# Key scores of the decoded samples computed beside the prompt's dilated attention instead of beside the gate units

## The chip, the core and the metric

The kernel runs on one NeuronCore of one Trainium2 chip. Its engines are named as the profile names them: PE (TensorE, with PEld for its weight loads), DVE (VectorE), ACT (ScalarE), POOL (GpSimd) and SP (SyncE, which here issues every DMA). The metric is the device time of one execution in microseconds (us), the median of three runs; less is better. The kernel before takes 921.87 us (908.17 to 929.16).

## The reference, cut to what matters

One decoder layer takes one prompt of 1024 tokens and 8 decoded samples of 4 tokens each (32 sample tokens, 1056 columns in all). One input projection feeds three groups of heads: retention, dilated sliding-window attention (8 heads of 64) and attention into 256 memory tokens. Each group has a gate, and one output projection with a layer norm closes the layer. For the samples, the sliding-window attention reads a cache of keys and values:

```python
def _dilated_sample(q, keys, vals, wb, dil, steps):
    idx = wb + jnp.arange(T)[:, None] - dil * jnp.arange(steps + 1)[None, :]
    kg = keys[:, idx_c]
    vg = vals[:, idx_c]
    s = jnp.einsum('bthd,btnhd->bthn', q, kg).astype(F32) * (D ** -0.5)
    ...
    p = jnp.exp(s - m[..., None])
    l = p.sum(-1)
    o = jnp.einsum('bthn,btnhd->bthd', p, vg.astype(F32)) / l[..., None]
```

The change is about `s`, the scores of these cached keys. The kernel gets them in two ways: the last 128 positions of a sample on PE, and six classes of older positions, which only one of the four tokens reads, as a product of a cached key row with the query (on POOL) and a sum over 64 elements (on DVE).

## The kernel before, in words

The engines' programs are written in source order; nothing reorders them. The main loop goes through `UNITS`, each a projection of 256 columns: `mq`, `mk`, `mv` (memory), `qk` and `vr` (sliding-window queries and keys; values of both groups), `rq`, `rk` (retention), and the gates `rg`, `mg`, `sg`. `accumulate` (L213) issues a unit's matmuls, three per block of 128 rows since each factor is split into a high and a low part, and yields after every two blocks (six matmuls). At each yield `pump` gives credit to two streams of generators, `fa` and `fb`, by `RATE` (a pair for each unit, halved); a whole credit runs one step. So PE sees six or more matmuls of a unit, then a few of a stream's step, and so on.

- `fa` carries the memory attention, then `swa_prompt` (the prompt's dilated attention), then at unit `("mg", 0)` `ret_prompt` (retention in 8 chunks), `ret_sample` and `mem_sample`.
- `fb` carries what the samples need in the sliding-window group: `keys`, `softmax` and, during the output projection, `values` (all in `swa_sample`). Before the change, `keys` is added at `("mg", 0)`, so it runs beside retention; `softmax` follows in `("sg", 0)` and `("sg", 1)`.

A step of `swa_prompt` issues scores on PE (L521), mask and row maximum on DVE (L523), exp on ACT (L529). Later `factor` (L546 to L554, small DVE operations on tiles `sf`) merges the denominators of two patterns, which travel through DRAM (`st_d`, `so`), then `weigh` (L561, POOL) scales the scores, `trans` (L571, L576, PE) transposes them, and `av` (L600, PE) multiplies by the values. Query tiles `q` come back from DRAM (`hl_d`) by SP just ahead of use.

In retention, for each chunk of 128 tokens, `inner` issues PE L703 and L706, then DVE L709 (the masked scores `sm`) and an ACT copy. `outer` issues PE L723, L725, L728, an ACT copy, then DVE L735 (the state `R`) and `norm_sums`: DVE L794, L796, `rsqrt` (DVE L782, then POOL L783, a power), DVE L798. `apply` (ACT L803) of a chunk stands behind the next chunk's `outer`, and `finish` (PE transposes L747) three chunks later. `inner` of a chunk takes both buffers of pool `ps_s`, so it waits for DVE L709 of the chunk before it. DVE runs in order: whatever stands behind L798 waits for POOL's L783.

In `keys`, each of the 16 steps before the change has a POOL product L1059 on a tile of 128 x 1536 and, one step later, a DVE sum L1038:

```python
load_cl(d["swa_kc"], n + CL_LEAD)
pr = cl.pop((b, x))
product(n, K_POOL)(out=pr, in0=pr, in1=qb_t[b][:, None, :].to_broadcast([128, 3, 512]), op=ALU.mult)
```

Dense scores are PE L1046 and L1052. `softmax` calls `nc.gpsimd.partition_all_reduce` twice (L1101 maximum, L1116 sum). In the built program, POOL gets an instruction that loads another library of POOL code (MODIFY_POOL_CONFIG in the trace, a bare `ISA` row in the order of instructions) wherever the next operation isn't in the one at hand: the all-reduce is in one, the ordinary elementwise operations are in another.

Of the kernel before, what the change touches and what calls it, by code (L numbers as in the profile page):

```python
# [18 lines left out]
NS = 32  # L19
# [19 lines left out]
P_BUFS = 8  # L39
# [12 lines left out]
CL_LEAD = 1  # L52
# [43 lines left out]
def trunk_kernel(ctx: ExitStack, tc: tile.TileContext, d):  # L96
# [68 lines left out]
    def close(es):  # L165
        flush_stores()
        es.close()
# [798 lines left out]
    def swa_sample():  # L966
# [5 lines left out]
        qf, kf = one([128, 4, NS], "qf"), one([128, 4, NS], "kf")  # L972
# [4 lines left out]
        cm, mp, mx, sel = one([128, 4, 8, 2], "cm"), one([128, 64, 4], "mp"), one([128, 64, 4], "mx"), one([128, 64, 4], "sel")  # L977
# [3 lines left out]
        cl, qb_t, dn = {}, {}, {}  # L981
        HB = [(b, x) for b in range(8) for x in range(2)]

# [6 lines left out]
        def load_dense(src, b):  # L990
            if b < 8:
                dn[b] = clp.tile([128, 512], F32, tag="dn", name="dn")
# [8 lines left out]
        def product(n, pattern):  # L1001
            return (nc.gpsimd if pattern[n % len(pattern)] else nc.vector).tensor_tensor

        def keys():
            load(qf, qs_d[:, 0:64].rearrange("u p t c -> (p t) u c"))
            load(kf, qs_d[:, 64:128].rearrange("u p t c -> (p t) u c"))
            for n in range(CL_LEAD):
                load_cl(d["swa_kc"], n)
            load_dense(d["swa_kd"], 0)
            load_dense(d["swa_kd"], 1)  # L1010
# [6 lines left out]
            load_qb(0)  # L1017
            load_qb(1)
# [10 lines left out]
            for u in range(4):  # L1029
                nc.vector.tensor_tensor(out=En[:, u].rearrange("p b (g i) -> p b g i", g=2), in0=sn[0:NS, u * 64:(u + 1) * 64].rearrange("p (b g i) -> p b g i", b=8, g=2),  # L1030
                                        in1=mask_n[:, :, None, :].to_broadcast([NS, 8, 2, 4]), op=ALU.add)
            yield
            last = None

            def reduce():
                if last is not None:
                    b, x, pr = last
                    nc.vector.tensor_reduce(out=Ec[:, b, 3 * x:3 * x + 3].rearrange("p c h -> p (c h)"),  # L1038
                                            in_=pr.rearrange("p c (h e) -> p (c h) e", e=64), axis=AX.X, op=ALU.add)

            for n, (b, x) in enumerate(HB):
                reduce()
                if x == 0:
# [5 lines left out]
                elif b % 4 == 3:  # L1049
# [11 lines left out]
                if x == 1:  # L1061
                    load_dense(d["swa_kd"], b + 2)
                    load_qb(b + 2)
# [31 lines left out]
        def softmax():  # L1095
            nc.vector.tensor_tensor(out=Ec, in0=Ec, in1=mask_c[:, None, :, None].to_broadcast([128, 8, 6, 8]), op=ALU.add)
# [38 lines left out]
        def values():  # L1135
            for n in range(V_LEAD):
                load_cl(d["swa_vc"], n)
            load_dense(d["swa_vd"], 0)
            load_dense(d["swa_vd"], 1)
# [12 lines left out]
            for n, (b, x) in enumerate(HB):  # L1152
                if x == 0:
                    for u in range(4):
                        nc.tensor.matmul(out_of(b, u), lhsT=quarter(EdU, b, u), rhs=dn[b][:, u * 128:(u + 1) * 128], start=False, stop=False)
                    load_dense(d["swa_vd"], b + 2)
# [7 lines left out]
            ut = one([128, 4, NS], "ssu")  # L1164
# [181 lines left out]

    avail = set()
    v_used = {}
    for u, (kind, j) in enumerate(UNITS):
# [4 lines left out]
        if (kind, j) == ("vr", 0):  # L1354
# [3 lines left out]
            swa_es = ExitStack()  # L1358
# [24 lines left out]
        if (kind, j) == ("mg", 0):  # L1383
            fa.drain()
            close(swa_es)
            ret_es, cl_es, ms_es = ExitStack(), ExitStack(), ExitStack()
            sw1 = pool(cl_es, "sw1", 1)
# [4 lines left out]
            def const_in(name, p):  # L1392
                sizes = [math.prod(SHAPES[k][1:]) for k in PACK[name]]
                t = p.tile([128, sum(sizes)], F32, name=name)
                load(t, d[name])
                out, at = [], 0
                for k, n in zip(PACK[name], sizes):
                    rows, *shape = SHAPES[k]
                    keys = " ".join("abc"[:len(shape)])
                    out.append(t[0:rows, at:at + n].rearrange(f"p ({keys}) -> p {keys}", **dict(zip("abc", shape))))  # L1400
                    at += n
                return out

            mask_n, mask_d, mask_c, cls_m, ind, decay = const_in("sw_c", sw1)
            ss_keys, ss_softmax, ss_values = swa_sample()
            fb.add("sk", ss_keys())
# [51 lines left out]
        avail.add((kind, j))  # L1458
        if kind == "mq":
            fa.add(("mem", j), mem_prompt(j))  # L1460
# [279 lines left out]
```

## Time and profile before

| | us |
|---|---|
| median of three runs | 921.87 (908.17 to 929.16) |
| the profiled execution, as timed | 920.39 |
| its span, first to last instruction | 918.6 |
| PE busy | 860.4 (94%) |
| DVE busy | 467.5 (51%) |
| ACT busy | 309.0 (34%) |
| POOL busy | 243.6 (27%) |

The profiled execution is 1.5 us faster than the median and 1.8 us longer than its span. PE's busy time counts matmuls that overlap in its pipeline, so a busy PE isn't necessarily a PE at its peak, and the clock that it is granted has two levels, 2.4 GHz (1.00 in the rows) and 1.2 GHz (0.50). Of the stretches that matter here, the prompt's dilated attention runs up to 523 us, retention (units `mg` and the start of `sg`) from 523 to 670 us, the samples' memory attention to about 717 us, and the output projection after 731 us.

### The profile page before, as it was taken

What the parts mean: (1) busy time and instruction counts of PE and PEld (TensorE: products, weight loads), DVE (VectorE), ACT (ScalarE), POOL (GpSimd) and SP (SyncE); (2) the same over time, 40 slices, a digit from 0 to 9 for tenths busy, and PEclk for the clock granted to TensorE, in tenths of its full rate; (3) what the DMA queues carried; (4) which work ended last, traced back from release to release, by engine and by line L of the source; (5) the groups of instructions that cost most, each with busy time, mean ns of one, the idle gap of its engine ahead of it and who ended that gap; (6) DMA issues with size and microseconds to landing.
All of it is one profiled execution on the core that took longest, in us unless ns stands there. A gap on an engine that the chain in (4) does not pass through costs nothing.

```text
span 918.6 us, 16177 instructions
## 1 busy us (share of the span) xinstructions
PE 860.4 (94%) x6034; PEld 766.9 (83%) x6034; DVE 467.5 (51%) x1048; ACT 309.0 (34%) x863; POOL 243.6 (27%) x249
## 2 busy tenths in 40 slices
PE   7999999999998999999999889977799988899996
PEld 6999999999997989899999778766685866677786
DVE  5566355155334535563344347885544446455534
ACT  5545235244333433342454233432212431001100
POOL 0004023024302421343022214574510202234310
PEclk9999999999998999999999989988699999999999
DMA  8565333875448436655554267749377777998430
GB/s 255 178 200 152 106 107 113 218 186 123 111 107 212 124 95 151 156 137 158 130 127 124 76 200 248 236 133 294 125 283 253 201 254 252 328 301 303 140 82 29
DMA packets 141646, 160.92 MB, mean 175 GB/s; under 512 B 39232, under 2 KB 102592, under 8 KB 141568
## 3 DMA queue, kind: packets, MB, share of 16 engines
q1 hardware_dynamic: 141568, 159.89, 58.7%
q8 instruction: 48, 0.79, 0.4%
q14 instruction: 30, 0.25, 0.1%
HBM read 120.59 MB, written 39.26 MB: 174 GB/s over the span
## 4 chain that ended last, share of the span: by engine, by line
PE 70%; DMA 14%; DVE 6%; ACT 3%; issue 3%; SPq 2%; POOL 1%; POOLq 0%; ACTq 0%; DVEq 0%
PE pp L222 37%; PE pp L1489 12%; PE s L521 4%; PE o L600 3%; DMA q<-hl_d 3%; DMA wr<-in_w_out 2%; SPq L160 2%; DMA s<-in_xT 2%; DMA cl<-in_swa_vc 2%; PE tp L571 1%; PE s L1160 1%; PE s L397 1%; DVE wl L173 1%; PE pp L1524 1%; DMA ut_d<-um 1%
## 5 line engine op out<-in xcount | busy, mean ns | idle before, releaser
L222 PE MATMUL pp<-xh,wh 128*128 128x352 f32 x672 | 232.1, 345 | 5.3 <-ACT xh L170 5.2
L222 PE MATMUL pp<-xh,wl 128*128 128x352 f32 x672 | 222.2, 331 | 0.2 <-DVE wl L173 0.2
L222 PE MATMUL pp<-xl,wh 128*128 128x352 f32 x672 | 222.3, 331 | 0.0
L222 PEld LDWEIGHTS pp<-xh,wh 128*128 128x128 f32 x672 | 131.4, 196 | 16.7 <-issue 9.5
L222 PEld LDWEIGHTS pp<-xl,wh 128*128 128x128 f32 x672 | 131.6, 196 | 0.8 <-DVE xl L173 0.8
L222 PEld LDWEIGHTS pp<-xh,wl 128*128 128x128 f32 x672 | 131.2, 195 | 0.4 <-DVE wl L173 0.4
L173 DVE TENSOR_TENSOR wl<-wr,wh 128x512 fp32r<-128x512 f32 (+1 forms) x113 | 84.0, 754 | 87.7 <-ACT wh L170 86.9
L561 POOL TENSOR_TENSOR pt<-pt,sf 128x256 f32<-128x256 f32 (+1 forms) x128 | 70.6, 585 | 168.0 <-DVE sf L554 161.8
L529 ACT ACTIVATE pt<-pt,sw 128x256 f32<-128x256 f32 (+1 forms) x128 | 59.6, 467 | 78.0 <-DVE sw L523 77.1
L1489 PE MATMUL pp<-wh,mh 128*128 128x512 f32 x192 | 79.6, 415 | 5.1 <-ACT mh L170 2.6
L1489 PE MATMUL pp<-wl,mh 128*128 128x512 f32 x192 | 77.5, 404 | 0.8 <-DVE wl L173 0.7
L170 ACT ACTIVATE wh<-wr 128x512 fp32r<-128x512 f32 (+1 forms) x113 | 69.0, 622 | 25.1 <-DMA wr<-in_w_out 23.0
L1489 PE MATMUL pp<-wh,ml 128*128 128x512 f32 x192 | 77.3, 403 | 0.1
L222 PE MATMUL pp<-wh,xh 128*128 128x256 f32 x256 | 74.9, 293 | 0.0
L222 PE MATMUL pp<-wl,xh 128*128 128x256 f32 x256 | 72.2, 282 | 0.0
L222 PE MATMUL pp<-wh,xl 128*128 128x256 f32 x256 | 72.1, 282 | 0.0
L523 DVE CUSTOM_DVE_ANT_0 pt<-s,mask 128x256 f32<-128x256 f32 (+1 forms) x128 | 43.1, 379 | 42.7 <-PE s L521 36.2
L521 PE MATMUL s<-k,q 128*128 128x256 f32 (+1 forms) x256 | 56.3, 356 | 7.5 <-DMA q<-hl_d 6.2
L1059 POOL TENSOR_TENSOR cl<-cl,qb 128x1536 f32<-128x1536 f32 x16 | 55.4, 3481 | 14.5 <-DMA cl<-in_swa_kc 9.0
L521 PEld LDWEIGHTS s<-k,q 128*128 128x128 f32 x256 | 51.0, 262 | 9.2 <-issue 4.7
L170 ACT ACTIVATE mh<-mraw 128x512 fp32r<-128x512 f32 (+1 forms) x27 | 15.9, 594 | 109.8 <-POOL mraw L1213 109.7
L1489 PEld LDWEIGHTS pp<-wh,mh 128*128 128x128 f32 x192 | 37.0, 193 | 17.7 <-ACT wh L170 3.6
(238 smaller groups left out, 1481.0 us busy)
## 6 DMA issues: line engine op xcount, KB each, us to landing
wr<-in_w_in SPq DMA_DIRECT2D x87, 256.0 KB, 3.7
cl<-in_swa_kc SPq DMA_DIRECT2D x16, 768.0 KB, 6.2
cl<-in_swa_vc SPq DMA_DIRECT2D x16, 768.0 KB, 7.0
hl_d<-hl SPq DMA_DIRECT2D x24, 352.0 KB, 2.9
q<-hl_d SPq DMA_DIRECT2D x32, 256.0 KB, 4.8
tab<-in_tabs SPq DMA_DIRECT2D x18, 352.0 KB, 3.3
gt_d<-t SPq DMA_DIRECT2D x36, 176.0 KB, 5.2
wr<-in_w_out SPq DMA_DIRECT2D x24, 256.0 KB, 5.2
```

Source lines behind the costliest of these rows:

```text
L160: nc.sync.dma_start(out=out, in_=in_)
L170: nc.scalar.activation(out=out, in_=in_, func=copy, **kw)
L173: (nc.gpsimd if pool else nc.vector).tensor_tensor(out=out, in0=raw, in1=hi.bitcast(F32), op=ALU.subtract)
L222: nc.tensor.matmul(out, lhsT=a, rhs=b, start=(n == 0), stop=(n == 3 * KD - 1))
L397: nc.tensor.matmul(ps[:, i], lhsT=a, rhs=b[:, h, :], start=(n == 0), stop=(n == 2))
L521: nc.tensor.matmul(ps[:, out], lhsT=Q[h, b][:, x, q], rhs=K[h][:, k], start=(x == 0), stop=(x == 1))
L523: nc.vector.tensor_tensor_reduce(out=pt[:, out], in0=ps[:, out], in1=mask[:, msk], scale=1.0, scalar=3.0e38, op0=ALU.add, op1=ALU.min, acc ...
L529: nc.scalar.activation(out=pt[:, out], in_=pt[:, out], func=exp, scale=-1.0, bias=st[:, s, i, 0:1], accum_out=st[:, s, i, 1:2])
L561: nc.gpsimd.tensor_tensor(out=pt[:, out], in0=pt[:, out], in1=f[:, 0, 4 * s + i, None].to_broadcast([128, n]), op=ALU.mult)
L600: nc.tensor.matmul(o[64 * g:64 * g + 64, col:col + 128], lhsT=v, rhs=pt[:, at:at + 128], start=g not in begun, stop=last and final[g] == n)
L1059: product(n, K_POOL)(out=pr, in0=pr, in1=qb_t[b][:, None, :].to_broadcast([128, 3, 512]), op=ALU.mult)
L1489: nc.tensor.matmul(ps, lhsT=a[:, k], rhs=b[k, c], start=(n == 0), stop=(n == 35))
```

## The change

Unit `("qk", 3)` moves ahead of `("rk", 0)`, and at its end, when the queries of all sample heads exist, `keys` is added to `fb`. It runs during `rk`, `vr`, `rg` and `rg` at new rates, in 24 steps on tiles of 128 x 1024 with a pool of its own (`kcp`), and must be done at `("mg", 0)`. There `softmax` is added, so that it now runs beside retention's first chunks. `P_BUFS` (score tiles of the prompt's attention) falls from 8 to 7. Constants for the samples are loaded at `("vr", 0)`.

```diff
 UNITS = (
...
-    + [("qk", 2), ("vr", 2), ("rk", 0), ("qk", 3), ("vr", 3), ("rg", 0), ("rg", 1)]
+    + [("qk", 2), ("vr", 2), ("qk", 3), ("rk", 0), ("vr", 3), ("rg", 0), ("rg", 1)]
...
-P_BUFS = 8
+P_BUFS = 7
...
-CL_LEAD = 1
+KC_LEAD = 1
...
-    ("vr", 0): (0.8, 0), ("rq", 0): (0.95, 0), ("vr", 1): (0.65, 0), ("qk", 2): (0.95, 0), ("vr", 2): (0.8, 0), ("rk", 0): (0.7, 0),
-    ("qk", 3): (0.95, 0), ("vr", 3): (0.4, 0), ("rg", 0): (0.9, 0), ("rg", 1): (0.7, 0), ("mg", 0): (1.1, 0.7), ("mg", 1): (0.9, 0.7),
+    ("vr", 0): (0.8, 0), ("rq", 0): (0.95, 0), ("vr", 1): (0.65, 0), ("qk", 2): (0.95, 0), ("vr", 2): (0.8, 0), ("rk", 0): (0.7, 0.5),
+    ("qk", 3): (0.95, 0), ("vr", 3): (0.4, 0.5), ("rg", 0): (0.9, 0.6), ("rg", 1): (0.7, 0.6), ("mg", 0): (1.1, 0.7), ("mg", 1): (0.9, 0.7),
...
+        def load_kc(n):
+            if n < 24:
+                b, x = KB[n]
+                kc[b, x] = kcp.tile([128, 2, 512], F32, tag="kc", name="kc", bufs=3)
+                load(kc[b, x], d["swa_kc"][b, :, 2 * x:2 * x + 2])
...
-                qb_t[b] = clp.tile([128, 512], F32, tag="qb", name="qb", bufs=3)
+                qb_t[b] = kcp.tile([128, 512], F32, tag="qb", name="qb", bufs=2)
...
-            for n, (b, x) in enumerate(HB):
+            for n, (b, x) in enumerate(KB):
                 reduce()
-                if x == 0:
+                if x == 0 and b:
+                    load_qb(b + 1)
+                if x == 1:
...
-                load_cl(d["swa_kc"], n + CL_LEAD)
-                pr = cl.pop((b, x))
-                product(n, K_POOL)(out=pr, in0=pr, in1=qb_t[b][:, None, :].to_broadcast([128, 3, 512]), op=ALU.mult)
+                load_kc(n + KC_LEAD)
+                if x == 2:
+                    load_dense(kcp, d["swa_kd"], b + 1)
+                pr = kc.pop((b, x))
+                nc.gpsimd.tensor_tensor(out=pr, in0=pr, in1=qb_t[b][:, None, :].to_broadcast([128, 2, 512]), op=ALU.mult)
...
         if (kind, j) == ("mg", 0):
             fa.drain()
+            fb.finish("sk")
             close(swa_es)
+            close(kc_es)
...
-            fb.add("sk", ss_keys())
             fb.add("sx", ss_softmax())
...
         avail.add((kind, j))
+        if (kind, j) == ("qk", 3):
+            fb.add("sk", ss_keys())
```

On POOL, from the last scaling of the prompt's scores (`pt`, L561) to the first products of the output stage (`mraw`): `rs` is retention's power, one for each chunk, `cl` a key product, `mx` an all-reduce of the samples' softmax, and a bare `ISA` a change of library. Before:

```order
L561 TENSOR_TENSOR pt<-pt,sf 128x256 x8
L783 TENSOR_TENSOR rs<-rs,nhalf 128x4 x2
L1059 TENSOR_TENSOR cl<-cl,qb 128x1536
...
L783 TENSOR_TENSOR rs<-rs,nhalf 128x1
L1059 TENSOR_TENSOR cl<-cl,qb 128x1536 x3
L907 MEMSET msq 128x1024
L909 MEMSET mspm 128x512
L1101 ISA
L1101 ISA mx<-mp 128x256
L1116 ISA mx<-mp 128x256
L1213 ISA
L1213 TENSOR_TENSOR mraw<-mraw,mg 128x512 x6
```

The same stretch of the changed kernel, where `kc` is the smaller key product and L1112 and L1127 are the two all-reduces:

```order
L1071 TENSOR_TENSOR kc<-kc,qb 128x1024
L561 TENSOR_TENSOR pt<-pt,sf 128x256 x8
L1112 ISA
L1112 ISA mx<-mp 128x256
L783 ISA
L783 TENSOR_TENSOR rs<-rs,nhalf 128x4 x2
L1127 ISA
L1127 ISA mx<-mp 128x256
L783 ISA
L783 TENSOR_TENSOR rs<-rs,nhalf 128x4 x6
L783 TENSOR_TENSOR rs<-rs,nhalf 128x1
```

The key products have left retention; in their place four changes of library stand among the powers of its first three chunks, where before two stood behind all of them.

On DVE, one chunk of retention in the middle of unit `("mg", 0)` (`mv` the scale and shift of the norm, `sm` the masked scores, `R` the state, `Ec` the sum of a key product). Before:

```order
L798 SCALAR_TENSOR_TENSOR mv<-mv,rs 128x4
L709 TENSOR_TENSOR sm<-s,ret_c 128x256 x2
L1038 TENSOR_REDUCE Ec<-cl 128x24
L302 SCALAR_TENSOR_TENSOR t<-t,pp 128x352
L173 TENSOR_TENSOR wl<-wr,wh 128x512
L735 TENSOR_TENSOR R<-o,R 128x256
```

In the changed kernel, around the sum that the second all-reduce waits for (`mp`) and the power behind it:

```order
L1126 TENSOR_TENSOR mp<-mp,En 32x256
L735 TENSOR_TENSOR R<-o,R 128x256
L794 BN_STATS bn<-hn 128x6 x4
L796 BN_AGGR mv<-bn 128x2 x4
L782 TENSOR_SCALAR rs<-mv 128x4
L798 SCALAR_TENSOR_TENSOR mv<-mv,rs 128x4
L709 TENSOR_TENSOR sm<-s,ret_c 128x256 x2
```

The sums of the key products are gone from here and parts of the softmax have come; `sm` still stands right behind L798.

On SP, at the start of unit `("rg", 0)`, where the last pair of heads begins (`q` a query tile, `vc` values, `st_d` denominators on their way out, `wr` weights). Before:

```order
L160 DMA vc<-vs_d_88 128x512
L160 DMA q<-hl_d_84 64x2x512 x2
L160 DMA wr<-in_w_in 128x512 x2
L535 DMA st_d_0_113<-sw 128x4x2
L535 DMA st_d_1_114<-sw 128x8
```

In the changed kernel, where `kc` are cached keys, `dn` the dense keys and `qb` a query broadcast to all partitions:

```order
L160 DMA vc<-vs_d_88 128x512
L160 DMA wr<-in_w_in 128x512
L160 DMA q<-hl_d_84 64x2x512 x2
L160 DMA kc<-in_swa_kc 128x1024
L160 DMA dn<-in_swa_kd 128x512
L160 DMA qb<-qt_d 32x512 x4
L160 DMA kc<-in_swa_kc 128x1024
L160 DMA wr<-in_w_in 128x512
L535 DMA st_d_0_113<-sw 128x4x2
L535 DMA st_d_1_114<-sw 128x8
```

Seven transfers of the keys have come between the query tile and the denominators.

## Rows read from the trace of the kernel before

**Rows 1.** The page: the TensorE clock granted in 40 slices of 23 us (9 is 90% or more of full speed).

```profile
PEclk9999999999998999999999989988699999999999
```

**Rows 2.** Busy time by stretch: stretch and its length, busy us (x instructions) of PE, PEld, DVE, ACT, POOL, then granted clock, share of the DMA engines, GB/s. The first is the end of the prompt's dilated attention, the others are retention.

```profile
447.00:525.00 78.00, 76.55 (x532) 70.94 (x531) 35.59 (x131) 33.19 (x103) 16.76 (x32) 1.00 0.44 111
525.00:560.00 35.00, 30.04 (x204) 25.41 (x203) 15.10 (x50) 10.62 (x28) 6.28 (x4) 0.85 0.70 218
560.00:615.00 55.00, 47.09 (x330) 38.27 (x328) 47.59 (x79) 21.00 (x56) 32.23 (x14) 0.93 0.65 209
615.00:670.00 55.00, 45.15 (x312) 38.94 (x311) 30.43 (x34) 13.70 (x35) 25.32 (x9) 0.73 0.54 175
```

**Rows 3.** The chain that ended last, 604 to 660 us, in order of time: start us, length us, what.

```profile
607.53 1.02 POOL rs L783
...
625.89 3.01 DMA k2s<-rk_d
...
629.04 0.43 PE s L823 x8
...
645.52 3.37 DVE mv L798
...
649.81 2.88 PE tp L871 x16
```

**Rows 4.** Groups of instructions, 525 to 730 us: line, engine, operation, tiles, shapes, count | busy us, mean ns of one | idle before them and what ended it.

```profile
L1059 POOL TENSOR_TENSOR cl<-cl,qb 128x1536 f32<-128x1536 f32 x16 | 55.4, 3481 | 14.5 <-DMA cl<-in_swa_kc 9.0 <-DVE wl L173 5.5
...
L798 DVE SCALAR_TENSOR_TENSOR mv<-mv,rs 128x4 f32<-128x4 f32 x8 | 24.0, 3003 | 9.5 <-POOL rs L783 9.5
```

**Rows 5.** DVE in order of time, during a key product that POOL runs from 569.74 us: start us, length us, what [idle before <- releaser].

```profile
569.81 3.39 DVE L798 SCALAR_TENSOR_TENSOR mv<-mv,rs 128x4 f32<-128x4 f32 x1 [1.21 <-POOL rs L783]
573.13 1.74 DVE L1038 TENSOR_REDUCE Ec<-cl 128x24 f32<-128x1536 f32 x1
```

**Rows 6.** POOL in order of time, same columns: eight scalings in the prompt's attention, and retention's power for the third chunk.

```profile
479.04 4.61 POOL L561 TENSOR_TENSOR pt<-pt,sf 128x256 f32<-128x256 f32 x8 [11.02 <-DVE sf L554]
...
559.18 1.01 POOL L783 TENSOR_TENSOR rs<-rs,nhalf 128x4 f32<-128x4 f32 x1 [6.94 <-ACT hn L803]
```

**Rows 7.** PE in order of time, either side of the wait at 645 us: in a run of like matmuls the distance of two starts is the price of one.

```profile
644.47 0.32 PE L222 MATMUL pp<-xl,wh 128*128 128x352 f32 x1
644.63 0.32 PE L222 MATMUL pp<-xh,wl 128*128 128x352 f32 x1
...
653.37 0.49 PE L222 MATMUL pp<-xh,wl 128*128 128x352 f32 x1
653.67 0.49 PE L222 MATMUL pp<-xh,wh 128*128 128x352 f32 x1
```

**Rows 8.** Changes of POOL's library (POOLq is POOL's sequencer): duration ns min/median/max, first and last start us.

```profile
L413 POOLq EVENT_SEMAPHORE  x11: 17/42/47157, 12.7 to 148.7; - x11
L413 POOLq MODIFY_POOL_CONFIG  x2: 11/11/11, 1.0 to 1.0; - x2
...
L1101 POOLq MODIFY_POOL_CONFIG  x2: 10/10/10, 675.6 to 675.7; - x2
L1101 POOL PARTITION_ALL_REDUCE mx<-mp x1: 1082/1082/1082, 685.5 to 685.5; - x1
...
L1213 POOLq EVENT_SEMAPHORE  x30: 17/43/12317, 709.1 to 886.0; - x30
L1213 POOLq MODIFY_POOL_CONFIG  x2: 88/88/88, 695.4 to 695.5; - x2
```

**Rows 9.** POOL's second all-reduce and, in the last line, the DVE operation that the first one waits for; columns as above.

```profile
693.69 1.80 POOL L1116 PARTITION_ALL_REDUCE mx<-mp  x1 [7.08 <-DVE mp L1115]
...
679.48 0.41 DVE L1100 TENSOR_TENSOR mp<-mp,En 32x256 f32<-32x256 f32 x1
```

**Rows 10.** The chain that ended last, 525 to 730 us: pieces of PE that make up a chunk of retention (12 matmuls of a gate unit; L703 and L706; from L723 to L728; L747), the keys' own (L1014, L1046, L1052), and L877, retention's last.

```profile
536.63 0.54 PE tp L1014 x4
537.17 1.93 PE pp L222 x12
539.10 0.65 PE s L703 x8
539.74 0.37 PE s L706 x2
...
554.14 0.30 PE o L723
...
556.27 0.61 PE o L728 x8
...
589.18 0.58 PE tp L747 x4
...
638.86 0.36 PE sd L1046 x8
...
668.59 0.21 PE tp L877
668.80 0.81 PE tp L1052 x8
```

**Rows 11.** A late query tile in the prompt's attention: a piece of the chain, and the stretch around it (columns as in the second group).

```profile
281.39 5.33 DMA q<-hl_d
...
275.00:300.00 25.00, 20.62 (x108) 19.73 (x107) 13.00 (x52) 10.52 (x37) 5.95 (x10) 0.86 0.80 197
```

More of the change, by code (lines that the diff above doesn't have):

```diff
@@ L970, in one, with late @@
             return sw1.tile(shape, F32, name=name)
-        qf, kf = one([128, 4, NS], "qf"), one([128, 4, NS], "kf")
+        def late(shape, name):
+            return clp.tile(shape, F32, name=name, bufs=1)
         qtok = one([128, 512], "qtok")
@@ L976, in swa_sample @@
         Wc = []
-        cm, mp, mx, sel = one([128, 4, 8, 2], "cm"), one([128, 64, 4], "mp"), one([128, 64, 4], "mx"), one([128, 64, 4], "sel")
+        cm = one([128, 4, 8, 2], "cm")
+        mp = mx = sel = None
         EnF = En.rearrange("p u b (g i) -> p (u b g) i", i=4)
@@ L980, in swa_sample @@
         EdU = Ed.rearrange("p (u b g) i -> p u b (g i)", u=4, g=2)
-        cl, qb_t, dn = {}, {}, {}
+        kc, cl, qb_t, dn = {}, {}, {}, {}
         HB = [(b, x) for b in range(8) for x in range(2)]
+        KB = [(b, x) for b in range(8) for x in range(3)]
         def load_cl(src, n):
@@ L996, in load_qb @@
             if b < 8:
-                qb_t[b] = clp.tile([128, 512], F32, tag="qb", name="qb", bufs=3)
+                qb_t[b] = kcp.tile([128, 512], F32, tag="qb", name="qb", bufs=2)
                 for r in range(4):
                     load(qb_t[b][32 * r:32 * r + 32], qt_d[4 * b + r].partition_broadcast(32))
-        def product(n, pattern):
-            return (nc.gpsimd if pattern[n % len(pattern)] else nc.vector).tensor_tensor
         def keys():
+            qf, kf = (kcp.tile([128, 512], F32, tag="qb", name=n, bufs=2)[:, 0:128].rearrange("p (u t) -> p u t", u=4) for n in ("qf", "kf"))
             load(qf, qs_d[:, 0:64].rearrange("u p t c -> (p t) u c"))
             load(kf, qs_d[:, 64:128].rearrange("u p t c -> (p t) u c"))
[L1007 to L1010, printed above, removed]
+            for n in range(KC_LEAD):
+                load_kc(n)
+            load_dense(kcp, d["swa_kd"], 0)
             yield
@@ L1095, in softmax @@
         def softmax():
+            nonlocal mp, mx, sel
+            mp, mx, sel = (late([128, 64, 4], n) for n in ("mp", "mx", "sel"))
             nc.vector.tensor_tensor(out=Ec, in0=Ec, in1=mask_c[:, None, :, None].to_broadcast([128, 8, 6, 8]), op=ALU.add)
@@ L1163, in values @@
                 yield
-            ut = one([128, 4, NS], "ssu")
+            ut = late([128, 4, NS], "ssu")
             tp = ps_t.tile([128, 512], F32, tag="t", name="tp")[:, 0:256].rearrange("p (b u g i) -> p b u g i", b=8, u=4, g=2)
@@ L1345, in pump, with const_in @@
         fb.pump(b)
+    def const_in(name, p):
+        sizes = [math.prod(SHAPES[k][1:]) for k in PACK[name]]
+        t = p.tile([128, sum(sizes)], F32, name=name)
+        load(t, d[name])
+        out, at = [], 0
+        for k, n in zip(PACK[name], sizes):
+            rows, *shape = SHAPES[k]
+            keys = " ".join("abc"[:len(shape)])
+            out.append(t[0:rows, at:at + n].rearrange(f"p ({keys}) -> p {keys}", **dict(zip("abc", shape))))
+            at += n
+        return out
     avail = set()
@@ L1390, in trunk_kernel @@
             rtp = pool(ret_es, "rtp", 2)
[L1392 to L1405, printed above, removed]
-            fb.add("sk", ss_keys())
             fb.add("sx", ss_softmax())
```

31 lines of the change are left out of this document (16 added, 15 removed).

## The prediction

> **What bounds the kernel now.** I read the clock line of the page first: it is full except for a dip near 290 us, at the start of retention and in its second half [rows 1]. The table of stretches says what lies behind it [rows 2]. At the end of the prompt's dilated attention PE is busy 76.6 of 78 us at full clock: that stretch is bound by PE, and what is put there must hide or it costs. Retention is different. From 525 to 670 us PE is idle for 4.96 + 7.91 + 9.85 = 22.7 of 145 us, and its clock averages 0.85, 0.93 and 0.73. DVE is busiest in the middle, 47.6 of 55 us.
>
> The groups say with what [rows 4]. Eight DVE operations L798 on 4 elements a partition take 24.0 us, 3.0 us each. The timeline shows why [rows 5]: L798 starts as POOL starts a key product (3.48 us on the mean) and ends with it, while the sum L1038, which reads one tile, starts and runs as usual behind it. So the key products stop DVE operations that read two tiles of SBUF, and L798 stands in retention's own chain. The chain of waits shows the same for the samples' retention: L798 at 645.52 us takes 3.37 us, PE waits until 649.81 [rows 3], and then runs at 0.30 us a matmul instead of 0.16 [rows 7] until 668.6 us [rows 10].
>
> **What the changed retention costs.** PE's own work for a chunk is two gate pieces of 1.93, L703 and L706 1.02, L723 to L728 556.27 + 0.61 - 554.14 = 2.74, and L747 0.58: 8.2 us [rows 10]. Before, five chunks took 607.53 - 559.18 = 48.4 us, 9.7 each [rows 3, 6]. That difference, the late sample part and the low clock are what leaves with the products.
>
> Something else comes in. The order shows four changes of POOL's library among the powers of the first three chunks. What one costs is in the trace three times [rows 8]. After the one at 1.0 us the sequencer's next act is at 12.7 (11.7 us); after the one at 695.4 it is at 709.1 (13.7 us); after the one at 675.6 the all-reduce begins at 685.5 (9.9 us), though what it waits for on DVE was done at 679.89 [rows 9], so the load is worth at least 5.6 us. I take 9.9 us into the all-reduce's library and 12.7 us (the mean of the two others) back. None of this is hidden as it was before, when POOL had nothing due.
>
> I walk through PE's order from the second chunk's L703, t = 0, which stands at 529.3 us now and, since retention's first loads and the drain of the attention ahead are the same, there again.
> - The first load runs while POOL is idle: free. The all-reduce ends near t = 4; the load back 12.7 later at 16.7; the first chunk's power (1.0), L798, the masked scores and the normalization that L747 needs follow by t = 20. PE gets to the place that needs them (L703 of chunk 3, counted from 0, and L747 of chunk 0) at 1.0 + 1.9 + 2.1 + 1.9 + 1.0 + 1.9 + 2.7 + 1.0 = 13.5, with 2 us more for the low clock at the start. Wait: 4.5 us.
> - The second chunk's power is done near t = 26. Then 9.9 load, 1.8 all-reduce [rows 9], 12.7 load, 1.0 power [rows 6]: 51. With L798, the masked scores behind it and the normalization: 53. PE, from 20 on, has 1.6 + 1.9 + 2.7 + 1.9 + 1.6 + 1.9 + 2.7 + 1.9 = 16.2 us of work before L703 of chunk 5, whose two score buffers wait for the masked scores of chunk 4 behind that L798. Wait: 53 - 36.5 = 16.5 us. DVE, held in order at L798, holds gate and weight work as well.
> - The rest of the chunks is 28 us (three at 8.2 and the open one), the end up to L823 another 12 (42 gate matmuls at 0.16, two pieces and the last transposes), and the low clock after the wait 4 (some 8 us of it; 19 us followed the wait at 645, so this is an estimate).
> - The sample part took 668.6 - 629.0 = 39.6 us. It loses the wait of 4.9 us at 645, 18.8 x (1 - 0.16 / 0.295) = 8.6 of low clock, and two dense scores and more (0.9): 25.
> Sum: 53 + 28 + 12 + 4 + 25 = 122, so L877 at 651 instead of 668.6. I take a gain of 16 us. The ends: if a load costs 5.6 us, the first wait goes and the second is 5, 18 us better; at nothing 25 better; at 13.7 each 6 worse.
>
> A rule of the Trainium skill lies between (GPSIMD Engine Reference, section 2.1, Instruction dispatch): the first call to freshly loaded POOL code pays about 6 us for the load, beyond the wait for its data. The 5.6 us from DVE's last operation to the all-reduce agree with it, while the 11.7 and 13.7 us before the sequencer's next act do not. By the page the two waits would be some 15 us shorter and the time near 899.
>
> **What the prompt's attention pays.** The keys' PE work comes here: eight dense scores of 0.36 (2.9), L1014 and L1027 (0.54 and about as much), two L1052 (0.81 at low clock, about 0.45 here): 4.9 us, all on the path, since PE is full. POOL gets 24 products of 128 x 1024, by length 3.48 x 2/3 = 2.3 us, 55 us in all. Nine of them fall in the stretch of 78 us where POOL has 16.8 busy: 38 of 78. DVE gets 24 sums of 1.74 x 2/3 = 1.2 us, and products may hold its two-tile operations (factors, weights) for up to 2.3 us each: 35.6 + 11 + 21 = 67 of 78 us. Neither is full, but both stand in the chain from denominators to transposes: factor on DVE, scaling on POOL (4.61 us for eight [rows 6]), transposes on PE one step later. A scaling behind a product comes up to 2.3 us late. SP gets 24 + 8 + 32 loads and some more; the order shows seven of them between a query tile and the denominators, and each new load of a broadcast query waits for POOL's product of the step before, with the attention's transfers behind it. A wait for a query tile has a row: the chain waits 5.33 us there, PE idles 4.4 of 25 us, and the clock falls to 0.86 [rows 11]. From nothing (all in PE's shadow) to 20 us (four such, with their clock) is possible; I take 5, nearer to nothing, since the products run in small pieces and half of them fall where no scaling is due.
>
> The swap of the two units moves the same work, and `P_BUFS` of 7 leaves PE the same attention steps in the drain at `("mg", 0)`: nothing, at most 2 either way. The softmax leaves `sg`, where it delayed nobody: nothing.
>
> **Sum.** 920.4 - 16 + 4.9 + 5 = 914 us against the profiled execution's 920.4 (1.5 below the median): 0.6% faster. A measurement of this kernel can tell about 2%, so this is no change.
>
> **Rivals.**
> - *The loads of POOL's code cost little.* Then the products' going is nearly all gain: at 5.6 us each 896, at nothing 889; I name 896. For it: only one of the three intervals ends in an operation, and data came late there. Against it: the sequencer's own silence of 11.7 and 13.7 us. 0.27.
> - *The attention's chain becomes the bound.* From unit `rk` on, each of the five remaining pairs of head and half waits for its scaling or query tile: a product ahead (2.3), a factor held by one (2.3), and half speed after it (7 us at 0.5 in the stretch of rows 11, 3.5 lost): 8 us each, 40 in all, 914 - 5 + 40 = 949. It decides the sign where the five cost over 11 us, 2.3 each, about one product. For it: PE has no slack there. Against it: POOL and DVE are half idle, and a step lies between scaling and transposes. 0.17.
> - *The clock takes the gain back.* The waits of 4.5 and 16.5 us keep PE at 1.2 GHz as the wait at 645 did, through the sample part too: 8.6 of low clock stay and 4 come in the chunks, 927. The change then moves retention's waits without removing them. 0.10.
>
> **How the numbers follow.** My forecast has 0.46 and by itself runs from 905 to 926 (prompt waits 0 to 12, loads 5 us either way). The wide range takes in 896 with some of its spread and the milder half of the second rival: 894 to 934. Faster by over 2% is the first rival and a little of the forecast's tail: 0.29; slower by over 2% the second and a little more: 0.18; the rest, 0.53, lies within.
>
> **What would show it.** Right: no L798 near 3 us; a hole in PE and DVE of 10 to 20 us once, early in retention, that ends with the third chunk's power; 20 to 26 us between the powers of chunks 1 and 2, and chunks after it at 8 to 8.5 us; L877 some 15 us nearer to retention's start; the stretch before it about 10 us longer. Wrong: the powers of chunks 1 and 2 less than 15 us apart (first rival); PE idle for more than 15 us before retention (second); a clock below 0.8 through the sample part (third).

## The result

The changed kernel is slower by 1.05% (ratio 1.0105, interval 1.0073 to 1.0137; medians 924.8 us beside 916.1, 20 runs each). The ratios here and below go by fast runs alone and are not the quotients of the medians, from which they differ by up to 0.8%. The forecast was 914 us, 0.6% faster. Its profiled execution took 924.36 us (span 922.6) beside 920.39, so the two traces differ by 4.0 us, less than the medians; what follows goes by stages of the traces, with the ratios beside them.

The stages, from the first and last starts of their lines: retention's first L703 at 523.2 us before and 554.0 after (30.8 later); from there to L823, where the samples' part begins, 105.8 and 87.5 (18.3 less); the samples' part up to L877 39.4 and 28.1 (11.3 less); from L877 to the end 250.2 and 253.0. The sum is 4.0. The cost was forecast at 10, the gain of the two retention stages at 16.

The clock line of the page after, which answers to [rows 1]:

```profile
PEclk9999999999999999999998989899999998899999
```

The dips have moved from 570 to 690 us to 500 to 600, into the prompt's attention and retention's start. The stretches after (columns as in [rows 2]): the one that was full before, the whole of the prompt's end, and retention in two parts.

```profile
447.00:525.00 78.00, 65.78 (x436) 61.46 (x435) 50.51 (x117) 26.65 (x89) 40.68 (x30) 0.91 0.84 232
447.00:554.00 107.00, 91.81 (x621) 82.49 (x619) 68.94 (x154) 36.21 (x114) 56.31 (x49) 0.90 0.68 188
554.00:610.00 56.00, 47.52 (x316) 38.79 (x316) 26.60 (x94) 18.15 (x47) 8.00 (x7) 0.88 0.40 107
610.00:670.00 60.00, 56.85 (x451) 49.83 (x450) 21.55 (x71) 28.77 (x76) 4.20 (x5) 0.97 0.36 112
```

PE was busy 76.6 of 78 us there before and 65.8 now, at 0.91 instead of full clock. Neither DVE (50.5 of 78) nor POOL (40.7) is full. So it is waits, and the largest is this one. POOL after, in order of time (start us, length us, what [idle before <- releaser]):

```profile
472.16 2.40 POOL L1071 TENSOR_TENSOR kc<-kc,qb 128x1024 f32<-128x1024 f32 x1 [0.96 <-DVE sw L523]
485.40 2.34 POOL L1071 TENSOR_TENSOR kc<-kc,qb 128x1024 f32<-128x1024 f32 x1 [10.84 <-DMA kc<-in_swa_kc]
487.70 2.11 POOL L561 TENSOR_TENSOR pt<-pt,sf 128x128 f32<-128x128 f32 x4
```

DVE had the factor ready (its last operation, L554, starts at 480.43), but POOL stood 10.84 us at a product whose keys had not come, with the scaling behind it. SP, in order of time, had issued that load only behind the other pattern's denominators (`so`, for whose trip through DRAM SP waited 3.5 us) and the next keys and queries, and it landed 6 us after its issue:

```profile
470.82 1.36 SPq L149 DMA_DIRECT2D gt_d<-t  x1
475.76 0.92 SPq L160 DMA_DIRECT2D so<-st_d  x2
476.73 1.12 SPq L160 DMA_DIRECT2D k<-hl_d  x2
477.89 1.25 SPq L160 DMA_DIRECT2D q<-hl_d  x2
479.27 0.99 SPq L160 DMA_DIRECT2D kc<-in_swa_kc  x2
```

PE at the same time:

```profile
479.91 0.32 PE L222 MATMUL pp<-xh,wl 128*128 128x352 f32 x1
488.72 0.90 PE L571 MATMUL tp<-ident,pt 128*128 128x128 f32 x3 [8.49 <-POOL pt L561]
489.27 0.64 PE L222 MATMUL pp<-xh,wh 128*128 128x352 f32 x1
```

It stands still for 8.49 us and then pays 0.30 to 0.44 us a matmul instead of 0.16 for some 3 us. In all, POOL waited 39.4 us for key loads in this stage (groups of instructions, 400 to 554 us; columns as in [rows 4]):

```profile
L1071 POOL TENSOR_TENSOR kc<-kc,qb 128x1024 f32<-128x1024 f32 x24 | 57.6, 2404 | 42.2 <-DMA kc<-in_swa_kc 39.4 <-DVE sw L523 2.0 <-DVE t L302 0.7
```

In retention the products' hold is gone; the group that was 24.0 us in [rows 4] is now (554 to 670 us)

```profile
L798 DVE SCALAR_TENSOR_TENSOR mv<-mv,rs 128x4 f32<-128x4 f32 x8 | 1.3, 164 | 22.5 <-POOL rs L783 22.5
```

164 ns instead of 3003, and 15.0 of its 22.5 us of idle time (6.95 and 8.08) stand behind two powers that waited for POOL's changes of library. POOL after, in retention's first four chunks:

```profile
562.04 1.69 POOL L1112 PARTITION_ALL_REDUCE mx<-mp  x1 [13.64 <-issue]
571.64 1.05 POOL L783 TENSOR_TENSOR rs<-rs,nhalf 128x4 f32<-128x4 f32 x1 [7.92 <-issue]
579.58 1.01 POOL L783 TENSOR_TENSOR rs<-rs,nhalf 128x4 f32<-128x4 f32 x1 [6.89 <-DVE rs L782]
586.56 1.81 POOL L1127 PARTITION_ALL_REDUCE mx<-mp  x1 [5.97 <-issue]
596.06 1.05 POOL L783 TENSOR_TENSOR rs<-rs,nhalf 128x4 f32<-128x4 f32 x1 [7.69 <-issue]
602.20 1.01 POOL L783 TENSOR_TENSOR rs<-rs,nhalf 128x4 f32<-128x4 f32 x1 [5.09 <-DVE rs L782]
609.62 1.01 POOL L783 TENSOR_TENSOR rs<-rs,nhalf 128x4 f32<-128x4 f32 x1 [6.41 <-DVE rs L782]
617.61 1.01 POOL L783 TENSOR_TENSOR rs<-rs,nhalf 128x4 f32<-128x4 f32 x1 [6.98 <-ACT hn L803]
```

"issue" ahead of an operation with a change of library holds the load of its code: 5.97 us into the all-reduce's library, 7.92 and 7.69 back, each from the end of POOL's operation before (data came 4.5, 2.1 and 0.7 us into these). The powers of chunks 1 and 2 are 16.5 us apart (forecast 20 to 26), the next three 6.1 to 8.0 (forecast 8 to 8.5). The chain of waits shows the two holes as the only pieces of "issue" of any length:

```profile
565.79 5.85 issue
571.64 1.06 POOL rs L783
...
589.15 6.91 issue
596.06 1.06 POOL rs L783
```

### The profile page after: what moved, and what is told of

Same layout as the page of the kernel before. It is cut to its first block, busy times and chain, and to the rows that moved or that the text cites. A ratio compares the mean times of both kernels' runs of the same rounds, so it can differ in the third digit from the quotient of the medians.

```text
span 922.6 us, 16204 instructions
## 1 busy us (share of the span) xinstructions
PE 855.0 (93%) x6034; PEld 759.9 (82%) x6034; DVE 453.2 (49%) x1056; ACT 309.1 (34%) x863; POOL 244.8 (27%) x257
## 5 line engine op out<-in xcount | busy, mean ns | idle before, releaser
L173 DVE TENSOR_TENSOR wl<-wr,wh 128x512 fp32r<-128x512 f32 (+1 forms) x113 | 92.3, 826 | 85.6 <-ACT wh L170 78.1
L561 POOL TENSOR_TENSOR pt<-pt,sf 128x256 f32<-128x256 f32 (+1 forms) x128 | 70.2, 580 | 101.1 <-DVE sf L554 92.8
L1071 POOL TENSOR_TENSOR kc<-kc,qb 128x1024 f32<-128x1024 f32 x24 | 57.6, 2404 | 42.2 <-DMA kc<-in_swa_kc 39.4
L521 PE MATMUL s<-k,q 128*128 128x256 f32 (+1 forms) x256 | 55.6, 353 | 3.6 <-DVE sw L523 3.2
L1224 POOL TENSOR_TENSOR mraw<-mraw,mg 128x512 f32<-128x512 f32 (+1 forms) x27 | 40.6, 1522 | 54.3 <-DMA mraw<-ut_d 47.0
L521 PEld LDWEIGHTS s<-k,q 128*128 128x128 f32 x256 | 50.8, 260 | 4.5 <-DVE sw L523 3.4
L302 DVE SCALAR_TENSOR_TENSOR t<-t,pp 128x352 f32<-128x352 f32 x36 | 18.7, 520 | 71.3 <-ACT t L301 71.2
```

Of the source, the lines that this page charges most:

```text
L173: (nc.gpsimd if pool else nc.vector).tensor_tensor(out=out, in0=raw, in1=hi.bitcast(F32), op=ALU.subtract)
L302: nc.vector.scalar_tensor_tensor(out=g, in0=g, scalar=1.0, in1=ps, op0=ALU.add, op1=ALU.mult)
L521: nc.tensor.matmul(ps[:, out], lhsT=Q[h, b][:, x, q], rhs=K[h][:, k], start=(x == 0), stop=(x == 1))
L561: nc.gpsimd.tensor_tensor(out=pt[:, out], in0=pt[:, out], in1=f[:, 0, 4 * s + i, None].to_broadcast([128, n]), op=ALU.mult)
L1071: nc.gpsimd.tensor_tensor(out=pr, in0=pr, in1=qb_t[b][:, None, :].to_broadcast([128, 2, 512]), op=ALU.mult)
L1224: nc.gpsimd.tensor_tensor(out=raw, in0=raw, in1=g, op=ALU.mult)
```

## The experiments

Times are ratios to the kernel before, run on the same chip. The stages are those of the one profiled execution, in which equal work may differ by some us.

| kernel | ratio (interval) | first L703, us | L703 to L823 | L823 to L877 |
|---|---|---|---|---|
| before | 1 | 523.2 | 105.8 | 39.4 |
| after | 1.0105 (1.0073 to 1.0137) | 554.0 | 87.5 | 28.1 |
| loads only | 0.9856 (0.9759 to 0.9952) | 545.5 | 86.5 | 34.5 |
| products, no loads | 0.9989 (0.9951 to 1.0026) | 542.9 | 89.3 | 33.7 |
| no loads, no products | 0.9882 (0.9826 to 0.9937) | 542.6 | 88.5 | 27.5 |
| softmax late | 0.9886 (0.9810 to 0.9962) | 554.7 | 74.2 | 25.5 |
| no change of library | 0.9972 (0.9934 to 1.0009) | 557.6 | 74.5 | 27.9 |
| before, order and 7 tiles | 1.0087 (1.0047 to 1.0127) | 537.5 | 105.9 | 29.8 |
| before, order alone | 1.0144 (1.0091 to 1.0198) | 539.6 | 104.7 | 29.5 |
| before, 7 tiles alone | 1.0158 (1.0114 to 1.0201) | 546.4 | 101.8 | 35.7 |

The fourth column falls into three groups: 102 to 106 us with the key products in retention, 86 to 89 without them, 74 without the library changes too. The last column has no such order: the samples' part took 29.5 to 39.4 us with the products still beside it and 25.5 to 34.5 without them.

**Loads without products.**

```diff
-                nc.gpsimd.tensor_tensor(out=pr, in0=pr, in1=qb_t[b]..., op=ALU.mult)
-                    nc.vector.tensor_reduce(out=Ec[...], in_=pr..., op=ALU.add)
+            nc.vector.memset(Ec, 0.0)
```

> The changed kernel without the 24 key products on POOL and their 24 sums on DVE; the loads of the keys, the dense scores on PE and everything else stay (the older classes' scores are left out, zeros stand for them). In the changed kernel the way from the first gate block (460.7 us) to retention's first matmul (554.0 us) is 93.3 us, 21.5 more than before. Theory A (scalings of the prompt's scores stand in POOL's queue behind products, which wait for key loads that come late): the 21.5 us shrink to 5 at most, since PE's waits for L561 (16 us in the attention) go; time about 903 us (900 to 910). Rival B (the products themselves, by occupying POOL and holding DVE's two-tile operations): the same here, told apart by the next two runs. Rival C (the loads on SP and the keys' own matmuls on PE): no more than 5 us faster, 920 or above.

Measured: 0.9856, and the way from the first gate block to L703 86.0 us, not 77 at most. The total is well below the kernel after, as A and B have it, but 22.3 us of the lateness stay without any product: C holds for most of the prompt's part, though only in part by its reasons, as the runs further down show. PE still waits 8.4 us for L561 from 340 us on (after: 16.3).

**The loads issued by ACT, and two steps ahead.**

```diff
-                load(kc[b, x], d["swa_kc"][b, :, 2 * x:2 * x + 2])
+                nc.scalar.dma_start(out=kc[b, x], in_=d["swa_kc"][b, :, 2 * x:2 * x + 2])
```

> The changed kernel with the 24 loads of cached keys issued by ACT instead of SP, so that they no longer stand behind SP's waits; nothing else changes. Theory A (products wait for loads that SP issues late): POOL's idle time ahead of the key products, 39.4 us in the changed kernel, falls below 15, PE's waits for L561 from 16 to below 5 us, and the time by 8 to 18 us, to 907 to 917. Rival B (the products' own time and their hold on DVE): the time stays within 4 us of 925. Rival C (SP crowded by the loads, so that query tiles and denominators come late): faster too, by up to 10 us, but through shorter waits for query tiles, with POOL's idle time ahead of the products unchanged.

```diff
-KC_LEAD = 1
+KC_LEAD = 2
```

> The changed kernel with each load of cached keys issued two steps ahead instead of one, in the same three buffers (so a load may wait on SP for the sum just issued). Theory A: POOL's idle time ahead of the products falls from 39.4 to some 20 us and the time by 4 to 12 us, 912 to 920, unless SP's new waits for buffers delay the query tiles. Rival B: within 4 us of 925. If SP's waits decide, slower than 928.

Measured: 1.0097 (1.0050 to 1.0143) and 1.0138 (1.0093 to 1.0183), the same as the kernel after or a little slower; L703 starts at 559.2 and 555.3 us, no earlier. POOL's idle time for key loads fell from 39.4 only to 31.5 with ACT, and to 17.0 with the longer lead; the longer lead also halved PE's waits for L561. In exchange PE waited 8.7 us for the dense keys (after: 2.2). PE's waits with the longer lead, 395 to 560 us (us in total, times, longest):

```profile
PE sd L1056 <- DMA dn<-in_swa_kd: 8.7, 4, 4.6
PE tp L571 <- POOL pt L561: 7.2, 7, 2.8
```

Theory A in its simple form, "issue the loads earlier", falls: the wait changes its place. The times (926.7 and 928.1 us) are those of rival B, which the crossed runs below don't bear out for this stage.

**The softmax behind retention.**

```diff
-            fb.add("sx", ss_softmax())
...
         avail.add((kind, j))
+        if (kind, j) == ("mg", 1):
+            fb.add("sx", ss_softmax())
```

> The changed kernel with the samples' softmax added at the end of unit mg instead of its start, so that its two all-reduces and their four changes of library fall behind most of retention's powers; the keys stay beside the prompt's attention. If the changes of library cost retention what the prediction took (waits of 4.5 and 16.5 us): 12 to 21 us faster, 904 to 913. If they cost what the profile after shows (reloads of 6 to 8 us; PE's waits for L703 and L747 together 8.4 us and a clock of 0.67 for 15 us): 5 to 12 us faster, 913 to 920. If other work fills the holes: within 3 us of 925.

Measured: 0.9886 from three executions, 2.2% (20 us) below the kernel after by the ratios and 15 us by the medians, 909.7 us in all: faster than both, though by less than 2% beside the kernel before (916.6 on that chip). L703 to L823 falls from 87.5 to 74.2 us. The powers, POOL in order of time:

```profile
566.28 1.04 POOL L783 TENSOR_TENSOR rs<-rs,nhalf 128x4 f32<-128x4 f32 x1 [17.58 <-DVE rs L782]
574.03 1.01 POOL L783 TENSOR_TENSOR rs<-rs,nhalf 128x4 f32<-128x4 f32 x1 [6.71 <-DVE rs L782]
581.35 1.01 POOL L783 TENSOR_TENSOR rs<-rs,nhalf 128x4 f32<-128x4 f32 x1 [6.31 <-ACT hn L803]
589.87 1.01 POOL L783 TENSOR_TENSOR rs<-rs,nhalf 128x4 f32<-128x4 f32 x1 [7.51 <-ACT hn L803]
```

7.3 to 8.5 us apart, with no hole; the 9.7 of [rows 3, 6] were the products'. The size is that of the first line of the expectation, the forecast's.

**The same without changes of library.** It tells the library's load from the softmax's other work.

```diff
-            nc.gpsimd.partition_all_reduce(flat(mx), flat(mp), 128, ...)
+            nc.gpsimd.tensor_copy(out=flat(mx), in_=flat(mp))
```

> The changed kernel with POOL's two all-reduces replaced by plain copies on POOL, so that no library changes fall into retention (the softmax is then not summed over partitions); everything else of the softmax stays at the start of retention. If the changes of library are what the late softmax gained (16 us between L703's first and L877, 115.6 to 99.7): the same here, 98 to 102 us, and 907 to 912 in all. If the gain came from the softmax's DVE and ACT work leaving retention: 110 us or more there and 918 to 925 in all.

Measured: 0.9972, 1.3% (12 us) below the kernel after; L703 to L823 74.5 us beside 74.2 with the late softmax, and 102.4 up to L877, as the first line has it. The time, 915.2 us, misses that line's 907 to 912. So the 13 us that retention loses are the library's, with the little by which the all-reduces (1.69 and 1.81 us) outlast the copies (1.07 and 0.40). The 8 us (0.86%) by which the late softmax is better still lie elsewhere; which work they are was not tried.

**Loads and products crossed.**

```diff
-                load(kc[b, x], d["swa_kc"][b, :, 2 * x:2 * x + 2])
```

This line goes in both runs. The first also goes without products and sums, as above; in the second the products take three resident tiles of zeros in turn.

> The changed kernel without the key products, their sums and the 24 loads of cached keys (12.6 MB); zeros stand for the older classes' scores. The dense scores with their loads and the broadcast queries stay. Beside the run that kept the loads (retention's first matmul at 545.5 us, 22.3 later than before, 910.4 us): if the loads crowd the DMA engines and SP in the prompt's attention, that matmul comes at 530 to 536 us and the time is 6 to 14 us below 910. If the loads cost nothing: 545 and 910 again, and the 22 us are the keys' own PE work (5.7 us) and the small edits.

> The changed kernel with all key products and sums, but on three resident tiles of zeros instead of the 24 loaded ones: the loads of cached keys are left out. If the products hurt by making the prompt's scalings wait for late loads (PE's waits for L561 16 us in the changed kernel): those waits fall below 4 us, and retention's first matmul comes within 3 us of the kernel without loads and products. If the products hurt by their own time on POOL and by holding DVE (L173 takes 1546 ns beside them and 712 without): still 6 to 12 us later than there. Time 905 to 918 either way.

Measured, first L703: neither 542.6, loads alone 545.5, products alone 542.9, both 554.0. Each alone adds 3 us at most, both together 11.4. The run without either came as the second line of its expectation has it (542.6 and 909.6 us). So neither the bytes (loads alone cost no time that these runs can tell, 0.9856 beside 0.9882) nor POOL's and DVE's work bring those us in this stage, but their meeting. PE's waits for L561, from 240 us to L703, say how: 9.3 us with neither, 11.6 with loads, 9.8 with products (the expectation had 4 at most), 18.6 with both. Some 9 of the 11.4 us are thus scalings that come late behind products that wait for loads. In the whole time the products alone cost 1.1%, more than this stage shows. Their profiled execution has 6 us of it in the samples' part (33.7 beside 27.5; L877 takes 415 ns beside 271), but so has that of the loads alone; with one trace each that is not settled.

**The two small edits, in the kernel before.**

```diff
-    + [("qk", 2), ("vr", 2), ("rk", 0), ("qk", 3), ("vr", 3), ("rg", 0), ("rg", 1)]
+    + [("qk", 2), ("vr", 2), ("qk", 3), ("rk", 0), ("vr", 3), ("rg", 0), ("rg", 1)]
-P_BUFS = 8
+P_BUFS = 7
```

> The kernel before with only the small edits: unit qk 3 ahead of rk 0, and 7 score tiles instead of 8; keys and softmax stay where they were. The prediction priced these at nothing, at most 2 us: 914 to 919 us beside 916.6 for the kernel before, retention's first matmul at 523 us as before. Rival (the swap or the eighth tile is part of why the first gate block came 9.3 us late in the changed kernel, and still 8.1 late without products): that block at 455 us or later instead of 451.4, and the time 4 to 9 us above the kernel before.

> The kernel before with only the order of units changed (qk 3 ahead of rk 0), 8 score tiles as before. The two small edits together cost 0.87% (8 us), with PE's waits for the scalings L561 up from 0.3 to 9.6 us and retention's first matmul 14.3 us later (537.5). If the order is the cause: the time 6 to 10 us above the kernel before, waits for L561 of 6 us or more, the matmul at 533 to 538. If the tiles are: within 3 us of the kernel before, waits below 2 us, the matmul at 522 to 526.

> The kernel before with only 7 score tiles instead of 8, the order of units as before. If fewer tiles are the cause (scores of the next pair run less far ahead, so that scalings and transposes of a pair come closer together on POOL and PE): the time 6 to 10 us above the kernel before, PE's waits for L561 of 6 us or more, retention's first matmul at 533 to 538. If the order of units is: within 3 us, waits below 2 us, the matmul at 522 to 526.

Measured: together 1.0087, the order alone 1.0144, the tiles alone 1.0158. No key work has moved in these. With both, the first gate block starts at 455.1 us, so the rival's line came true and the prediction's didn't. Each costs by itself, 13 and 14 us where 6 to 10 were expected of the cause, and together they cost no more than either (the intervals overlap) and far less than the sum, so "order or tiles" was the wrong question. With the order alone 15.7 of the 16.4 us stand ahead of the first gate block (467.1 us instead of 451.4), with 7 tiles alone 8.3 of 23.2 (459.7). With 7 tiles PE's waits in the prompt's attention (240 to 545 us) are (same columns), where before it waited 0.2 us for L561:

```profile
PE tp L571 <- POOL pt L561: 17.0, 12, 7.0
PE s L521 <- DVE sw L523: 3.1, 1, 3.1
```

The longest of them, PE and then POOL in order of time:

```profile
474.65 1.16 PE L521 MATMUL s<-k,q 128*128 128x256 f32 x4
...
484.69 0.90 PE L571 MATMUL tp<-ident,pt 128*128 128x128 f32 x3 [6.97 <-POOL pt L561]
```

```profile
483.67 2.47 POOL L561 TENSOR_TENSOR pt<-pt,sf 128x128 f32<-128x128 f32 x5 [52.69 <-DVE sf L554]
```

`swa_prompt` issues scores only while fewer than `P_BUFS` tiles are held (L640). After those at 474.65 PE has 12 gate matmuls, then transposes that need the scaling, and POOL waits for DVE's factor. The denominators are not what the factor waits for: SP issued their way back (`so`) at 467.99, and they landed 2.4 us later at most. DVE, then ACT, then SP, each in order of time:

```profile
480.77 0.52 DVE L302 SCALAR_TENSOR_TENSOR t<-t,pp 128x352 f32<-128x352 f32 x1 [7.92 <-ACT t L301]
481.90 0.16 DVE L546 TENSOR_TENSOR sf<-sw,so 128x8 f32<-128x8 f32 x1
480.27 0.46 ACT L301 ACTIVATE t<-pp 128x352 f32<-128x352 f32 x1 [6.64 <-DMA gt_d<-t]
467.99 0.92 SPq L160 DMA_DIRECT2D so<-st_d  x2
471.46 0.59 SPq L149 DMA_DIRECT2D gt_d<-t  x1
```

The factor (from L546) stands on DVE behind a gate's operation, L302, which waits for ACT's L301, and that for a tile `t` whose store to `gt_d` landed 8.7 us after its issue. In the kernel before, the matching factor runs at 462.42, ahead of such a wait of L302 (4.44 us, at 469.98). With both edits, five of PE's waits are over 1 us: at two of them DVE does wait for the denominators (3.6 and 3.8 us), at the other three it is held by other work. So fewer tiles take away cover from more than one wait; why the factor comes to stand behind L302 was not traced further. With the new order alone the wait is another (L521 for DVE L277, 9.7 us, two times).

**The small edits undone in the changed kernel.** Two runs gave the tiles room by taking one of three key buffers.

```diff
-P_BUFS = 7
+P_BUFS = 8
...
-name="kc", bufs=3)
+name="kc", bufs=2)
```

> The changed kernel with the softmax late and 8 score tiles instead of 7 (two key tiles instead of three make the room), the new order of units kept. Beside the late softmax alone (909.7 us): if order and tiles act together as in the kernel before (order with 8 tiles 1.44%, with 7 tiles 0.87%): some 5 us slower, 912 to 917. If the tile count acts by itself: 900 to 906. If the products hide it: within 3 us of 909.7.

> The changed kernel with the softmax late, the old order of units and 8 score tiles (two key tiles instead of three make the room; the keys' rates in vr 3 and rg rise to 0.7 and 0.75, since they begin one unit later). Run alone, the order and the seventh tile cost 1.44% and 1.58%, together 0.87%. If those 8 us come back on top of the late softmax: about 902 us (896 to 906). If the products crowd the shorter way more than that (13 of them stand in one run on POOL ahead of a pair's scalings): 910 to 922. If the tables of the kernel before fit only a stream without the keys: 910, as with the late softmax alone.

Measured: 1.0134 (1.0023 to 1.0244) and 1.0219 (1.0151 to 1.0286), so 2.5 and 3.4% above the late softmax alone, on which both build; the second also takes back the order and raises two rates. They tell nothing of order and tiles: with two key buffers, POOL waits 51.5 us for key loads in the first, and in the second PE waits 18.5 us for dense keys and 10.3 for the queries. A run without any key tiles (diff as above, with the old order and 8 tiles):

> The changed kernel without key loads, products and sums (zeros stand for the older classes' scores), and in addition the old order of units and 8 score tiles; without the key tiles, these fit with nothing else changed. Beside the same kernel with the new order and 7 tiles (909.6 us, ratio 0.9882, retention's first matmul at 542.6 us): if the two small edits cost in the changed kernel what they cost in the kernel before (0.87%): ratio about 0.980, the matmul at 528 to 534. If they only cost there: the ratio within 0.4% of 0.988 and the matmul at 540 or later.

Measured: 0.9963 (0.9921 to 1.0005), L703 at 552.5. Neither line: undoing the edits costs 0.8% here instead of giving 0.9% back. PE waits 9.2 us at the keys' first transpose for the samples' queries, which are written at the end of the last `qk` unit and read back at once; with the new order it waits 2.3. Why the wait is longer with the old order is not shown.

**Half of the products on DVE.**

```diff
-                nc.gpsimd.tensor_tensor(out=pr, ...
+                (nc.vector if n % 2 else nc.gpsimd).tensor_tensor(out=pr, ...
```

> The changed kernel with the softmax late, and every second key product on DVE instead of POOL. If the products cost by standing ahead of the scalings in POOL's queue: PE's waits for L561 fall from 15 us to below 9, retention's first matmul comes 4 to 8 us earlier than 554.7, and the time is 902 to 907. If they cost by taking DVE's time (a product holds DVE's two-tile operations now, and would then take DVE itself): the same within 3 us, 907 to 913. If DVE becomes the bound of the prompt's attention: slower than 914.

Measured: 0.9894 (0.9834 to 0.9954), L703 at 552.9, waits for L571 13.3 us (13.5 with all on POOL): the same as the late softmax alone. Halving POOL's products doesn't halve the waits; one late load ahead of a scaling is enough (8.2 of the 13.3 us stand behind one product that waited 13.28 us for its keys). It is the second version that is faster than both kernels, by no more than the first.

## Why the prediction was wrong

**The step that failed** is the paragraph on the prompt's attention. It had 4.9 us of PE work, 5 of waits, and for the two small edits "nothing, at most 2 either way"; 30.8 us came. By the traces: the small edits alone bring 14.3 (537.5 - 523.2), the changed kernel without loads and products 19.4 (5.1 more, against the 4.9 for the keys' own matmuls), and loads with products 11.4 more. So the PE term fits, the waits were twice the 5 but within the stated 0 to 20, and the edits that were priced by counting work were off by their whole cost. "The same steps in the drain" holds for the count, not for the time: ahead of unit `mg` PE has the same 16 transposes to do without gate matmuls between, but takes 6.3 us before and 10.4 with the edits, where it waits 3.3 us for scalings; with the new order alone it takes 6.4. What the count left out is waits: PE's for L571's scalings went from nothing to 12.8 us. In the whole time the two edits cost 8 us (0.87%), since the trace with them has the shorter samples' part. That the 14.3 and 5.1 add up inside the changed kernel isn't shown: the quiet run with the edits undone came out slower, and what the edits cost there stays open. Shown is that order and tiles hang together (their costs don't add), and that either edit alone costs 1.4 to 1.6% in the kernel before.

**The products' hold on DVE** was read rightly, and its size nearly: with the library changes out of the way L703 to L823 shrinks from 105.8 to 74.2 us. The walk without loads gave 6.1 (to the second L703) + 97 - 25 = 78. What was misread is the samples' part: its 39.4 us with half clock [rows 10] were taken for the products' doing, but the kernels with the small edits alone, products and all, have 29.5 to 35.7. In the trace before, a product did hold the samples' one L798 for 3.36 us; in those three it takes 0.16, so it is a matter of when a product falls. By these traces some 4 to 10 us of that gain belong to this one execution of the kernel before, which is also 4 us above the median of 20 runs: luck of the trace that the forecast was built on.

**The changes of library** were placed rightly (before the powers of chunks 0 and 2, the second the longer) but priced too high: 9.9 and 12.7 us, of which 6.0 and 7.7 to 7.9 came. The interval of 9.9 in [rows 8] held 4.2 us until DVE's data, and the two behind the 12.7 end in an act of the sequencer, not in an operation. The walk had chunk 2's power end at 51 us after the second chunk's L703; it ended at 38 (597.1 - 559.1). The changes then took 13.3 us of retention instead of 25. The Trainium skill's rule (GPSIMD Engine Reference, section 2.1, Instruction dispatch: about 6 us for a first call) was nearer than the value taken: the way in agrees with it (5.97 us), the way back is longer (7.7 to 7.9).

**The rivals.** "The loads cost little" was half right on the loads (near 6, not nothing) and wrong on the time. "The attention's chain becomes the bound" is what happened, at 31 us instead of 45, and its sign came (PE idle 15.2 us from 447 to 554), but mostly through another door: its mechanism, a product ahead of a scaling, has 11.4 us, just past the 11 from which it was to decide the sign; it left out that a product may itself stand waiting for a load. "The clock takes the gain back" did not: the clock is 0.97 from 610 to 670 us, and the samples' part took 28.1 us (641.5 to 669.6; forecast 25).

By the traces, 21 us too little cost in the prompt's attention and 14 too little gain behind it, of which a part was luck, left the time 1.0% above the kernel before instead of 0.6% below it.

## What to carry to other kernels

A buffer count or the order of two units in a hand-scheduled stream is a term of the sum, not a footnote: ask which wait the held buffers cover, and time that edit alone before adding work. An in-order engine that is half idle is no free place if the guest waits for a DMA there, since the wait is handed on to all that is queued behind. Keep changes of GpSimd's library out of a stretch in which GpSimd's answers are due: moving the softmax behind retention turned the change from 1.0% slower into 1.1% faster (three executions, interval 0.4 to 1.9%).

## What the runs showed of the hardware

Between retention's powers, a change of POOL's library took 5.97 us into the all-reduce's library and 7.69 and 7.92 us back, from the end of POOL's operation before to the start of the next, whose data came within that time. Over the seven traces that have these changes there it was 5.8 to 6.2 us in and 7.0 to 8.4 back. Beside the key products a two-tile DVE operation of 128x512 (L173) took 1546 ns on the mean instead of 712, and 1460 with the products alone, which put the end of this stage off by 0.3 us: longer DVE operations were hidden there, late ones on POOL were not.
